# Two transformer blocks on one core: convolution steps of the vector engine issued in front of vector instructions that the kernel's own clock sees waiting

## The chip, the cores and the metric

The kernel runs on one core of one Trainium2 chip. The metric is the device time of one execution in microseconds (us); the median over several runs counts. Engines are named as the profile names them: PE (the matrix engine; PEld is its weight load), DVE (the vector engine), ACT (the scalar engine), POOL, SP (it issues most DMAs).

## The reference, cut to what matters

512 tokens of width 1024 go through two blocks. The first has a hybrid mixer (mLSTM and state space) and a convolutional feed-forward network; the change does not touch it. The second block begins with the stage that matters here:

```python
y = rmsnorm(h, norm_mix_g[l]) @ w_in[l]
q = partial_rotary(y[..., 0:D_ATT]...)          # 8 heads of 64
k = partial_rotary(y[..., D_ATT:2 * D_ATT]...)
v = y[..., 2 * D_ATT:3 * D_ATT]...
att = dilated_sliding_attention(q, k, v)
conv = conformer_conv(y[..., c0:c0 + D_CONV], y[..., c0 + D_CONV:c0 + 2 * D_CONV], ...)
h = h + jnp.concatenate([att, conv], axis=-1) @ w_out[l]
xk = (mn @ w_xk[l])...                           # keys and values of a memory of 256 tokens
xv = (mn @ w_xv[l])...
```

`conformer_conv` gates its input (a * sigmoid(g)), runs a depthwise convolution of 31 taps along the tokens, then a layer norm and a silu. Its result and that of the attention are the two halves of the input to `w_out`.

## The kernel before

The program is written out once, instruction by instruction, in Python; each engine then runs its instructions in the order in which they were written. Matrix products in fp32 quality are split: a weight block `raw` (128x1024) comes by DMA, ACT rounds it to `whi`, DVE writes the rest `wlo = raw - whi`, and activations are split the same way (`hh`/`hl`, `cath`/`catl`, `mnh`/`mnl`, `qkh`/`qkl`). Five weight blocks fit in the ring, so ACT makes a `whi` when PE has finished with the block five earlier.

What is written next is decided while the program is built. A class `Pace` keeps a modelled clock per engine: every call goes through `Engine.issue` (L342), which issues the instruction and then lets `Pace.note` (L297) advance the engine's clock to the time at which the operands are there, plus a cost. Foreground loops (`phaseB`, `phaseA`, `tokensA`) write matrix products. After every few of them `pump()` (L665) goes through a list of background generators and writes the next piece of each that is due: its operands are there by the model, and the modelled clock of its engines is at most a limit ahead of PE's. `fill()` and `flush()` write the weight splits.

The stage around the change stands from L2018 on. In the foreground: the convolution's input (`ag`), Q, K and V, the memory's keys and values (`w_xk_2`, `w_xv_2`), and `residual_rms("w_out_2", ...)` (L2072). In the background: `to_heads` (transposes and splits of Q and K), eight generators `dilated` (one head each; PE writes scores `p` into a bank of tag `at`, of which there are two, DVE adds `band` and takes the row maximum into `P`, ACT takes the exponent, PE transposes, and PE multiplies `PT` by `va`), `conv_array` (some even shifts of two of the four channel tiles, on PE, from `cuh`, `cul` and `dg`), and `conv31` (L1826):

```python
for n, d in enumerate(vec):
    w = col("conv_w", (15 + d) * 4 + ct)
    o, a = shifted(y, v, d)
    stt(o, a, w, o, op0=OP.mult, op1=OP.add)     # one convolution step
    ...
    if n % CONV_N == CONV_N - 1 or n == len(vec) - 1:
        yield
```

One step is one DVE instruction `cv<-a,cols,cv`; there are 106 of that form. After the last step comes the tail: PE transposes `cv` to tokens (`cva`), DVE takes mean and variance (`st`, `mv`), POOL the root (`rstd`), ACT normalizes `cva`, PE transposes back, ACT and DVE apply gain, tanh and gate, and split the result into `cath` and `catl`, the second half of `w_out`'s input. `conv31` is added with a limit of 2500 ns (`CONV_BACK`): `pump` writes no step while DVE's modelled clock is more than that ahead of PE's.

Of the kernel before, what the change touches and what calls it, by code (L numbers as in the profile page):

```python
# [68 lines left out]
CONV_AHEAD = 2  # L69
CONV_AT = 5  # L70
CONV_LATE = 2500.0
TOP = 0
RESTART = 0.0
ATT_AHEAD = 4

# [204 lines left out]
class Pace:  # L280
# [3 lines left out]
    def __init__(self):  # L284
        self.clock = {"PE": 0.0, "DVE": 0.0, "ACT": 0.0, "POOL": 0.0, "DMA": 0.0}
        self.wrote, self.read = {}, {}

    def when(self, a, eng="PE"):
        t, by = self.wrote.get(_name(a), (0.0, eng))
        if by == eng == "PE":  # L290
            return 0.0
        return t + LAG[by] + (100.0 if eng == "PE" else 0.0)
# [1 line left out]
    def ready(self, aps):  # L294
        return max([self.when(a) for a in aps] or [0.0])

    def note(self, eng, cost, outs, ins):  # L297
        t = max([self.clock[eng]] + [self.when(a, eng) for a in ins])
        for a in outs:
            for e in (() if eng == "PE" else (self.wrote.get(_name(a)),)) + (self.read.get(_name(a)),):  # L300
                if e and e[1] != eng:
                    t = max(t, e[0] + WAR * LAG[e[1]])
        if BANKED:
            for a in ins:
                e = self.read.get(_name(a))
                if e and e[1] != eng and _name(a).startswith("p_"):
                    t = max(t, e[0] + LAG[e[1]])
        t += cost
        self.clock[eng] = t
        for a in ins:  # L310
            self.read[_name(a)] = max(self.read.get(_name(a), (0.0, eng)), (t, eng))
        for a in outs:
            self.wrote[_name(a)] = (t, eng)


def _name(a):
    t = getattr(a, "tensor", None)
    return getattr(t if t is not None else a, "name", None)


def _is_ap(a):
    return hasattr(a, "shape") and _name(a) is not None


def _free(a):
    n = 1
    for k in tuple(a.shape)[1:]:
        n *= int(k)
    return n


class Engine:
# [5 lines left out]
    def __getattr__(self, name):  # L338
        call = getattr(self._eng, name)
        kind, pace = self._kind, self._pace  # L340

        def issue(*args, **kw):  # L342
            r = call(*args, **kw)  # L343
            aps = [a for a in args if _is_ap(a)] + [v for k, v in kw.items() if k != "accum_out" and _is_ap(v)]
            outs, ins = aps[:1], aps[1:]
            if _is_ap(kw.get("accum_out", 0)):
                outs = outs + [kw["accum_out"]]
            if name == "dma_start":
                n = _free(aps[0]) * int(tuple(aps[0].shape)[0]) * 4
                pace.note("DMA", n / 330.0, outs, ins)  # L350
                return r
            n = max(_free(a) for a in aps[:2]) if name in ("bn_stats", "tensor_reduce") else _free(aps[0])
            scal = sum(1 for a in ins[1:] if _free(a) == 1)
            if kind == "PE":
                fp32 = ins[0].dtype == F32
                if name == "transpose":
                    cost = 109.0
                elif fp32:
                    cost = 4.0 * max(n / 2.4 + 2.5, 27.0) * (0.5 if _free(ins[0]) == 64 else 1.0)
                else:  # L360
                    cost = n / 2.4 + 2.5 if n >= 256 else 213.0
            elif kind == "DVE":
                fast = name in ("tensor_scalar", "tensor_copy") and all(not _name(a).startswith("p_") for a in aps)
                cost = 66.0 + 61.0 * scal + n / (1.92 if fast else 0.96)
            elif kind == "ACT":
                cost = 80.0 + 93.0 * scal + n * 0.833
            else:
                cost = 520.0 if name == "tensor_tensor" else 100.0 + n
            pace.note(kind, cost, outs, ins)
            return r  # L370

        return issue
# [12 lines left out]
def two_blocks_kernel(ctx: ExitStack, tc: tile.TileContext, x, mem, wg, cols_d, rows_d, b_ada, s5p, wqk, small_d,  # L385
                      dil_d, rope_d, out, dbg=None, stop=None):
    pace = Pace()
# [14 lines left out]
    def uid(n):  # L402
        serial[0] += 1
        return f"{n}_{serial[0]}"

    def slot(name, dt=F32, w=512):
        return slots.tile([128, 520], dt, name=uid(name), tag="s")[:, :w]
# [16 lines left out]
    def f(ap):  # L424
        return ap.bitcast(F32)
# [28 lines left out]
    class Stream:  # L454
# [26 lines left out]
        def step(self):  # L481
            self._dma()
            e = PLAN[self.prep]
            t = self.raw.pop(self.prep)
            self.prep += 1
            if e[0] == "R":
                self._ada(e[1], e[2], [t[:, 512 * c:512 * c + 512] for c in range(2)])
                self.raws -= 1
            elif e[0] == "C":
                self._columns(e[1], e[2], t)  # L490
            else:
                ring = self.rings < RING
                if ring:
                    hi = wpool.tile([128, 1024], F32R, name=uid("whi"), tag="whi")
                    lo = wpool.tile([128, 1024], F32R, name=uid("wlo"), tag="wlo")
                    if len(self.when) >= RING:
                        pace.read[_name(hi)] = pace.read[_name(lo)] = (self.when[-RING], "PE")
                    act(hi, t, AF.Copy)
                    self.late.append((lo, t, f(hi), True))
                    hi, lo = ([v[:, 512 * c:512 * c + 512] for c in range(2)] for v in (hi, lo))  # L500
                    self.when.append(0.0)
                    self.rings += 1
                else:
                    hi, lo = ([slot("whs", F32R) for _ in range(2)] for _ in range(2))
                    for c in range(2):
                        act(hi[c], t[:, 512 * c:512 * c + 512], AF.Copy)
                    for c in range(2):
                        self.late.append((lo[c], t[:, 512 * c:512 * c + 512], f(hi[c]), c == 1))
                    self.extras += 1
                self.ready.append((e, hi, lo))  # L510
                self.out.append(len(self.when) - 1 if ring else None)
                if self.eager or LATE > 1e8:
                    self.flush(-1)
            self._dma()
# [106 lines left out]
    background, waiting, limit, loads = [], {}, {}, {}  # L621

    def add(g, backlog=BACKLOG, engines=("DVE", "ACT")):
        background.append(g)
        waiting[g], limit[g], loads[g] = None, backlog, engines
        return g
# [3 lines left out]

    def step(g):
        waiting[g] = None
        try:
            waiting[g] = next(g)
        except StopIteration:
            background.remove(g)
            del waiting[g]

    def vacant(tag):

        if len(banks[tag]) < BANKS[tag]:
            return 0.0
        o = banks[tag][-BANKS[tag]]
        t, by = max(pace.read.get(o, (0.0, "PE")), pace.wrote.get(o, (0.0, "PE")))
        return t + LAG[by] + 100.0

    def due(g):

        need = waiting[g]
        if callable(need):  # L650
            return 0.0 if need() else None
        if not need:
            return 0.0
        t = pace.ready([a for a in need if not isinstance(a, str)])
        return max([t] + [vacant(a) for a in need if isinstance(a, str) and a in BANKS])

    filler = []

    def top():

        for g in filler:
            while g in background and due(g) == 0.0 and busy(g) <= pace.clock["PE"] + limit[g]:
                step(g)

    def pump():  # L665
        moved = True
        while moved:
            moved = len(ws.ready) < FIRST and ws.fill()
            for g in list(background):
                t, pe = due(g), pace.clock["PE"]  # L670
                now = pe + SLACK
                if isinstance(waiting[g], list) and waiting[g][-1] in ("DVE", "ACT"):
                    now = max(now, pace.clock[waiting[g][-1]] + LEAD)
                if t is None or t > now or busy(g) > pe + limit[g]:
                    continue
                step(g)
                moved = True
                top()
                if RESTART and pace.clock["PE"] > pe + RESTART:
                    break  # L680
            moved = ws.fill() or moved
# [878 lines left out]
    for e in MIXER:  # L1560
        kind, i = e[0], int(e[1])
# [456 lines left out]
    ws.eager = "A" in EAGER  # L2018
    add(conv_array(), CONV_BACK)
    conv = add(conv31(), CONV_BACK, CONV_ON)  # L2020
    if TOP:
        filler.append(conv)
    for n, e in enumerate(ORDER2):
        if n == CONV_AT:
            limit[conv] = CONV_LATE
# [191 lines left out]
```

## Time and profile before

| | |
|---|---|
| time, median of 3 runs | 1681.92 us (1680.43 to 1681.93) |
| profiled execution, its own time | 1682.57 us |
| its span (first to last instruction) | 1680.8 us |
| PE busy | 1604.9 us, 95% |
| PE weight load busy | 1295.3 us, 77% |
| DVE busy | 988.2 us, 59% |
| ACT busy | 698.8 us, 42% |
| share of PE in the chain that ended last | 82% |

The span is 1.8 us shorter than the profiled execution's time; what lies around it is not in the trace. "Busy" counts an engine as busy while at least one of its instructions runs. In the page's strip of 40 slices one slice is 42 us.

### The profile page before, as it was taken

The page shows a single profiled execution, that of the slowest core. Times are in us where ns is not written, and L with a number is a line of the kernel's source. Part 1 is how long each engine was busy: PE and PEld are TensorE (multiplying, and loading weights), DVE is VectorE, ACT ScalarE, POOL GpSimd, SP SyncE. Part 2 cuts the span into 40 slices and gives each one's busy share as a digit, 9 for nine tenths or more (in the row PEclk, how much of TensorE's full clock was granted, in tenths as well). Part 3 has the DMA queues.
Part 4 walks back from the last instruction along what each step waited for, and adds up shares of the span by engine and source line. Part 5 has one row for each costly group of instructions (what it writes and reads, how often), then busy time and mean ns, then how long its engine had stood idle before and what let it go on. Part 6 is the DMA issues. An engine that isn't in the chain of part 4 may idle for free.

```text
span 1680.8 us, 20291 instructions
## 1 busy us (share of the span) xinstructions
PE 1604.9 (95%) x7788; PEld 1295.3 (77%) x7788; DVE 988.2 (59%) x1940; ACT 698.8 (42%) x1151; POOL 35.4 (2%) x59
## 2 busy tenths in 40 slices
PE   5999999999979999999989999976999999999998
PEld 3778777878868888888868877745888888888886
DVE  6687768687675365554585685475554543334343
ACT  4455644533253254223344446534644532323231
POOL 1000000000010000000010000000000000000000
PEclk9999999999989999999989999996999999999999
DMA  9322322474502343333422122320311323232321
GB/s 359 127 82 63 120 78 87 163 233 155 200 26 88 126 164 112 114 102 97 138 64 76 63 64 89 113 88 26 110 57 60 113 88 100 88 101 88 100 75 51
DMA packets 60953, 178.47 MB, mean 106 GB/s; under 512 B 6964, under 2 KB 12340, under 8 KB 60856
## 3 DMA queue, kind: packets, MB, share of 16 engines
q1 hardware_dynamic: 54288, 166.15, 30.4%
q10 hardware_dynamic: 6568, 11.02, 1.9%
q8 instruction: 61, 1.00, 0.3%
q14 instruction: 36, 0.29, 0.1%
HBM read 171.90 MB, written 5.24 MB: 105 GB/s over the span
## 4 chain that ended last, share of the span: by engine, by line
PE 82%; DVE 7%; ACT 3%; issue 2%; DMA 2%; ACTq 0%; POOL 0%; SPq 0%; DVEq 0%; POOLq 0%
PE p L343 82%; DVE cv L343 1%; DMA raw<-in_wg_dram 1%; DVE mx L343 1%; DVE wlo L343 1%; ACT whi L343 1%; DVE hl L343 0%; DMA xres<-in_x_dram 0%; DVE xcv L343 0%; DVE st L343 0%; DVE m L343 0%; ACT xn L343 0%; ACT hh L343 0%; DVE s5t L343 0%; DVE acc L343 0%
## 5 line engine op out<-in xcount | busy, mean ns | idle before, releaser
L343 DVE TENSOR_TENSOR wlo<-raw,whi 128x1024 fp32r<-128x1024 f32 x244 | 297.4, 1223 | 346.1 <-ACT whi L343 345.8
L343 PE MATMUL p<-hh,whi 128*128 128x512 f32 (+1 forms) x1112 | 427.8, 385 | 0.0
L343 PE MATMUL p<-hh,wlo 128*128 128x512 f32 (+1 forms) x1112 | 418.2, 376 | 0.0
L343 PE MATMUL p<-hl,whi 128*128 128x512 f32 (+1 forms) x1112 | 416.9, 375 | 0.6 <-DVE hl L343 0.6
L343 ACT ACTIVATE whi<-raw 128x1024 fp32r<-128x1024 f32 x244 | 256.2, 1055 | 329.9 <-PE p L343 279.9
L343 PEld LDWEIGHTS p<-hl,whi 128*128 128x128 f32 x1112 | 210.7, 190 | 41.2 <-issue 1.7
L343 PEld LDWEIGHTS p<-hh,wlo 128*128 128x128 f32 x1112 | 210.2, 189 | 41.5
L343 PEld LDWEIGHTS p<-hh,whi 128*128 128x128 f32 x1112 | 210.5, 189 | 40.4 <-issue 2.7
L343 PE MATMUL p<-whi,fh 128*128 128x512 f32 x408 | 161.0, 395 | 0.0
L343 PE MATMUL p<-whi,fl 128*128 128x512 f32 x408 | 160.9, 394 | 0.0
L343 PE MATMUL p<-wlo,fh 128*128 128x512 f32 x408 | 160.6, 394 | 0.0
L343 PEld LDWEIGHTS p<-wlo,fh 128*128 128x128 f32 x408 | 76.7, 188 | 18.2
L343 PEld LDWEIGHTS p<-whi,fl 128*128 128x128 f32 x408 | 76.6, 188 | 18.2
L343 PEld LDWEIGHTS p<-whi,fh 128*128 128x128 f32 x408 | 76.6, 188 | 18.0 <-DVE facc L343 0.2
L343 DVE SCALAR_TENSOR_TENSOR cv<-a,cols,cv 128x511 f32<-128x511 f32 (+14 forms) x106 | 78.3, 740 | 2.4
L343 DVE SCALAR_TENSOR_TENSOR fg<-p,cols,fg 128x511 f32<-128x511 f32 (+1 forms) x44 | 32.9, 749 | 49.4 <-ACT fg L343 48.6
L343 DVE TENSOR_TENSOR mf<-p,mf 128x512 f32<-128x512 f32 x48 | 32.1, 685 | 29.0 <-PE p L343 29.0
L343 ACT ACTIVATE junk<-mf 128x512 f32<-128x512 f32 x32 | 20.2, 630 | 65.9 <-DVE mf L343 65.9
L343 ACT ACTIVATE fg<-p,cols 128x512 f32<-128x512 f32 x22 | 17.1, 778 | 60.5 <-PE p L343 60.5
L343 PE MATMUL p<-small,xn 128*128 128x128 f32 x128 | 20.0, 295 | 22.2 <-DVE hl L343 8.7
L343 PE MATMUL p<-whi,hh 128*128 128x512 f32 x96 | 39.3, 409 | 0.0
L343 DVE SCALAR_TENSOR_TENSOR acc<-raw,silu_c,acc 128x512 f32<-128x512 f32 x56 | 38.6, 744 | 0.9 <-DMA raw<-in_wg_dram 0.9
(408 smaller groups left out, 2458.8 us busy)
## 6 DMA issues: line engine op xcount, KB each, us to landing
raw<-in_wg_dram SPq DMA_DIRECT2D x283, 512.0 KB, 3.6
rw<-in_wg_dram SPq DMA_DIRECT2D x32, 256.0 KB, 5.9
x<-in_x_dram SPq DMA_DIRECT2D x8, 256.0 KB, 5.3
xres<-in_x_dram ACTq DMA_DIRECT2D x8, 256.0 KB, 5.0
out_dram<-mf SPq DMA_DIRECT2D x8, 256.0 KB, 2.1
u_dram<-us ACTq DMA_DIRECT2D x4, 256.0 KB, 3.6
U<-u_dram SPq DMA_DIRECT2D x16, 64.0 KB, 4.0
wqk<-in_wqk_dram ACTq DMA_DIRECT2D x4, 256.0 KB, 2.9
```

Of the source, the lines that this page charges most:

```text
L343: r = call(*args, **kw)
```

## The change

`Engine.issue` now asks, before it issues a DVE instruction, how long DVE's modelled clock would stand still until that instruction's operands are there (`Pace.start`, split off from `note`). While that is over 600 ns (`GAP`), and the convolution's next step has its operands, the step is written first. The limit against PE's clock does not apply there. A generator that is itself being run is left alone. The switch `TOP`, which was off, is removed.

```diff
-TOP = 0
+GAP = 600.0
...
+    def start(self, eng, outs, ins):
...
+    def note(self, eng, cost, outs, ins):
+        t = self.start(eng, outs, ins) + cost
...
         def issue(*args, **kw):
-            r = call(*args, **kw)
             aps = [a for a in args if _is_ap(a)] + [v for k, v in kw.items() if k != "accum_out" and _is_ap(v)]
             outs, ins = aps[:1], aps[1:]
...
+            if kind == "DVE" and pace.idle:
+                pace.idle(lambda: pace.start(kind, outs, ins) - pace.clock[kind])
+            r = call(*args, **kw)
...
+    filler, gaps = [], []
+    within = []
+
+    def idle(wait):
+
+        if within:
+            return
+        within.append(1)
+        for g in gaps:
+            while g in background and due(g) == 0.0 and wait() > GAP and g not in running:
+                step(g)
+        within.clear()
...
     conv = add(conv31(), CONV_BACK, CONV_ON)
-    if TOP:
-        filler.append(conv)
+    gaps.append(conv)
```

All instructions of the program are the same ones, in the same number and sizes, on every engine. What differs is their order, from the last part of the convolution's input stage to the first half of `w_out`. The three places that follow are named by the tiles: `cv` is a channel tile of the convolution, `P` one tile of scores of a head, `wlo` a weight block, `ao` an attention output. (L343 became L353.)

On DVE before, the end of the convolution stands behind the last attention output; these are consecutive rows, from the last `ao` on, and 19 more steps follow them without a break:

```order
L343 TENSOR_TENSOR ao_9370<-p_9361,rs_9357 128x512
L343 TENSOR_TENSOR catl_9373<-ao_9370,cath_9372 128x512
L343 SCALAR_TENSOR_TENSOR cv_7700<-a_1382_7530,cols,cv_7700 128x500
L343 SCALAR_TENSOR_TENSOR cv_7700<-a_1382_7530,cols,cv_7700 128x499 x2
L343 TENSOR_TENSOR wlo_9387<-raw_9206,whi_9386 128x1024
L343 SCALAR_TENSOR_TENSOR cv_7700<-a_1382_7530,cols,cv_7700 128x498 x2
L343 SCALAR_TENSOR_TENSOR cv_7700<-a_1382_7530,cols,cv_7700 128x497 x2
L343 SCALAR_TENSOR_TENSOR cv_7985<-a_1396_7618,cols,cv_7985 128x511
L343 TENSOR_TENSOR wlo_9422<-raw_9235,whi_9421 128x1024
L343 SCALAR_TENSOR_TENSOR cv_7985<-a_1396_7618,cols,cv_7985 128x511
L343 SCALAR_TENSOR_TENSOR cv_7985<-a_1396_7618,cols,cv_7985 128x509 x2
```

On DVE in the changed kernel the last step (shape 128x497) stands between two score tiles of the seventh head, with a step in front of almost every score tile:

```order
L353 TENSOR_TENSOR wlo_8864<-raw_8506,whi_8863 128x1024
L353 ISA P_8880,sm_8838<-p_8876,band_7221 128x512
L353 ISA sm_8838 128x1
L353 TENSOR_SCALAR sm_8838<-sm_8838 128x1
L353 SCALAR_TENSOR_TENSOR cv_7854<-a_1396_7620,cols,cv_7854 128x498
L353 ISA P_8916,sm_8838<-p_8912,band_7222 128x512
L353 ISA sm_8838 128x1
L353 TENSOR_SCALAR sm_8838<-sm_8838 128x1
L353 SCALAR_TENSOR_TENSOR cv_7854<-a_1396_7620,cols,cv_7854 128x497 x2
L353 TENSOR_TENSOR wlo_8931<-raw_8657,whi_8930 128x1024
L353 ISA P_8962,sm_8838<-p_8958,band_7223 128x512
```

Counted over the whole program: before, 55 steps stand ahead of the first score tile on DVE, 11 between the first and the last of the 32, and 40 behind the last; in the changed kernel 69, 37 and none. Between the first step and that last step stand 20 `wlo` instructions; the next is the 21st.

On PE before, the transposes of `cv` stand behind the last product of `w_out` that needs only the attention (`cath_9372` is the last attention output), all 16 in one piece:

```order
L343 MATMUL p_9377<-whi_9202,cath_9372 128x512
L343 MATMUL p_9377<-wlo_9203,cath_9372 128x512
L343 MATMUL p_9377<-whi_9202,catl_9373 128x512
L343 MATMUL p_9452<-small,cv_7516 128x128
L343 MATMUL p_9452<-small,cv_7519 128x128
L343 MATMUL p_9452<-small,cv_7700 128x128
L343 MATMUL p_9452<-small,cv_7985 128x128
```

On PE in the changed kernel they stand in groups of four between products of the memory's values (`mnh`, `mnl`) and transposes of the last head's `P`:

```order
L353 MATMUL p_9297<-small,cv_7516 128x128
L353 MATMUL p_9297<-small,cv_7519 128x128
L353 MATMUL p_9297<-small,cv_7703 128x128
L353 MATMUL p_9297<-small,cv_7854 128x128
L353 MATMUL p_9194<-whi_9180,mnh_5386 128x512
L353 MATMUL p_9194<-wlo_9181,mnh_5386 128x512
L353 MATMUL p_9194<-whi_9180,mnl_5390 128x512
```

Behind the fourth such group come, before the first transpose of `cva`: 24 products of 128x512, four transposes of `P`, four small products of `rs`, and the eight products `PT` by `va` of the last pair of heads. From there to the first product with the convolution's `cath`: the 16 transposes of `cva` and 30 products of 128x512.

## Rows read from the trace of the kernel before

**Rows 1.** The page: busy time of each engine, and PE's granted clock in 40 slices.
```profile
PE 1604.9 (95%) x7788; PEld 1295.3 (77%) x7788; DVE 988.2 (59%) x1940; ACT 698.8 (42%) x1151; POOL 35.4 (2%) x59
PEclk9999999999989999999989999996999999999999
```
**Rows 2.** Stretches: length, busy us (instructions) of PE, PEld, DVE, ACT, POOL, clock, DMA.
```profile
880.00:1121.40 241.40, 241.40 (x1288) 188.83 (x1288) 150.45 (x298) 120.14 (x229) 0.00 (x0) 1.00 0.25 82
1121.40:1160.40 39.00, 12.64 (x43) 8.72 (x42) 27.24 (x43) 14.89 (x22) 1.01 (x1) 0.56 0.07 25
1160.40:1201.80 41.40, 41.40 (x224) 35.40 (x223) 17.77 (x32) 20.67 (x39) 3.12 (x4) 1.00 0.27 87
```
**Rows 3.** Timeline of PE: start, length, instruction, count [idle before, until what].
```profile
1121.36 0.38 PE L343 MATMUL p<-small,cv 128*128 128x128 f32 x2
1123.68 0.33 PE L343 MATMUL p<-small,cv 128*128 128x128 f32 x1 [1.94 <-ACT cv L343]
1142.46 3.13 PE L343 MATMUL p<-small,cv 128*128 128x128 f32 x13 [18.45 <-ACT cv L343]
1149.71 0.48 PE L343 MATMUL p<-small,cva 128*128 128x128 f32 x1 [4.12 <-ACT cva L343]
...
1155.67 0.79 PE L343 MATMUL p<-whi,cath 128*128 128x512 f32 x1 [0.81 <-ACT cath L343]
```
**Rows 4.** Timeline of DVE: the 21st `wlo`, and the last convolution steps.
```profile
1060.95 1.22 DVE L343 TENSOR_TENSOR wlo<-raw,whi 128x1024 fp32r<-128x1024 f32 x1 [2.10 <-ACT whi L343]
...
1124.59 17.06 DVE L343 SCALAR_TENSOR_TENSOR cv<-a,cols,cv 128x511 f32<-128x511 f32 x22
...
1161.62 0.69 DVE L343 TENSOR_TENSOR catl<-cv,cath 128x512 fp32r<-128x512 f32 x1 [0.70 <-ACT cath L343]
```
**Rows 5.** Timeline of PE at full clock: eight transposes, their successor; products after the hole.
```profile
1080.37 1.04 PE L343 MATMUL p<-small,P 128*128 128x128 f32 x8
1081.33 0.49 PE L343 MATMUL p<-qkh,qkh 64*128 64x512 f32 x1
...
1160.35 0.39 PE L343 MATMUL p<-whi,cath 128*128 128x512 f32 x1
...
1161.05 0.39 PE L343 MATMUL p<-whi,cath 128*128 128x512 f32 x1
```
**Rows 6.** Stretches, for instructions on `cv` alone: PE, PEld, DVE, ACT, clock, DMA.
```profile
895.00:988.00 93.00, 0.00 (x0) 0.00 (x0) 40.72 (x55) 3.23 (x5) 1.00 0.27 85
988.00:1060.00 72.00, 0.00 (x0) 0.00 (x0) 7.34 (x10) 0.71 (x1) 1.00 0.23 74
1060.00:1121.40 61.40, 0.04 (x1) 0.18 (x2) 11.85 (x17) 0.00 (x0) 1.00 0.32 104
1121.40:1142.00 20.60, 0.67 (x3) 0.23 (x2) 18.42 (x25) 1.04 (x2) 0.62 0.14 47
```
**Rows 7.** Stretches ahead of the hole, all instructions, columns as in Rows 2.
```profile
895.00:940.00 45.00, 45.00 (x215) 37.44 (x214) 30.84 (x39) 19.89 (x36) 0.00 (x0) 1.00 0.30 93
940.00:988.00 48.00, 48.00 (x226) 38.92 (x224) 40.48 (x93) 20.05 (x40) 0.00 (x0) 1.00 0.24 78
988.00:1060.00 72.00, 72.00 (x423) 54.42 (x422) 40.92 (x104) 46.20 (x96) 0.00 (x0) 1.00 0.23 74
```
**Rows 8.** Waits, 895 to 1121.4: who waited for what, us in total, times, longest.
```profile
DVE wlo L343 <- ACT whi L343: 40.7, 24, 5.8
ACT P L343 <- DVE sm L343: 27.1, 22, 2.2
...
DVE P L343 <- PE p L343: 7.9, 10, 1.9
```

More of the change, by code (lines that the diff above doesn't have):

```diff
@@ L286, in __init__ @@
         self.wrote, self.read = {}, {}
+        self.idle = None
     def when(self, a, eng="PE"):
@@ L295, in ready @@
         return max([self.when(a) for a in aps] or [0.0])
-    def note(self, eng, cost, outs, ins):
+    def start(self, eng, outs, ins):
         t = max([self.clock[eng]] + [self.when(a, eng) for a in ins])
@@ L307, in note @@
                     t = max(t, e[0] + LAG[e[1]])
-        t += cost
+        return t
+    def note(self, eng, cost, outs, ins):
+        t = self.start(eng, outs, ins) + cost
         self.clock[eng] = t
@@ L632, in step @@
         waiting[g] = None
+        running.append(g)
         try:
@@ L637, in step @@
             del waiting[g]
+        finally:
+            running.remove(g)
     def vacant(tag):
@@ L655, in due @@
         return max([t] + [vacant(a) for a in need if isinstance(a, str) and a in BANKS])
-    filler = []
+    filler, gaps = [], []
[8 more added lines that the diff above has]
+        within.clear()
+    running = []
+    pace.idle = idle
     def top():
```

## The prediction

> **What bounds the kernel now.** I read the page first: PE is busy for 1604.9 of 1680.8 us, and the granted clock falls below full speed in only a few of the 40 slices, the deepest in the slice from 1134 to 1177 us [rows 1]. So PE sets the time nearly everywhere, and what an off-path change on DVE can give is PE's idle time. The second view is the split into stretches. From 880 to 1121.4 us PE is busy in all of 241.4 us at clock 1.00 while DVE works 150.45 us; from 1160.4 on it is busy all the time again. Between them lie 39 us in which PE does 12.64 us of work at a mean clock of 0.56 [rows 2]. That hole is the object of the forecast.
>
> The third view is PE's timeline through the hole. At 1121.36 PE has nothing left but transposes of `cv`; the fourth channel tile is not there. It waits 18.45 us until 1142.46 for ACT's last pass over `cv`, then 4.12 us for `cva`, and 0.81 us for `cath`, with which the products of `w_out` go on at 1155.67 [rows 3]. The wait named after ACT is DVE's: 22 convolution steps run in one piece from 1124.59, 17.06 us long, or 0.775 us a step [rows 4]. Of the 106 steps 25 lie inside the hole and only 27 between 988 and 1121.4 [rows 6], though DVE stood idle in 24 places ahead of a `wlo`, 40.7 us in all, between 895 and 1121.4 [rows 8]. The work that fills the hole existed earlier, and so did the room.
>
> **The change, part by part.** No instruction is added or removed, so only places count. By the order of instructions, 40 steps leave the end: 14 now stand ahead of the first score tile, 26 among the score tiles. The last step stands just ahead of the 21st `wlo`, whose twin ran at 1060.95 us before [rows 4], 60 us ahead of the hole. PE's transposes of `cv` stand among the products of the memory's values. Three terms follow.
>
> First, what the hole gives back. It runs from 1121.36 to 1160.35, where products reach their full pace, 38.99 us. What PE must still do of it: 32 transposes of `cv` and `cva`, and the first nine products of `w_out` with `cath`. At full clock eight transposes took 0.96 us, from 1080.37 to the next start at 1081.33, so 0.12 each and 3.84 for all; three products took 0.70 us from 1160.35 to 1161.05, so 0.233 each and 2.10 for nine [rows 5]. The gain is 38.99 - 3.84 - 2.10 = 33.05 us. Of it 2.6 us are the nine products alone, which ran at half rate behind the hole (1155.67 to 1160.35 is 4.68 us).
>
> Second, the tail behind the last step (statistics, root, normalization, gate, split). Its cover is the work that PE now has beside it. Before, PE's own part took 7.25 us from the first transposes of `cv` to the first of `cva` (1142.46 to 1149.71), 5.96 us on to the first product, and 12.6 us from 1149.71 to the end of the last `catl` at 1162.31 [rows 3, 4]. In the changed order there stand between the last transposes of `cv` and the first of `cva` 24 products (5.6 us), four transposes (0.5), four `rs` products and eight of `PT` by `va`; taking these twelve at no more than an ordinary product (2.8), that is 8.9 us, against the 7.25 that were needed. To the first product with the convolution's `cath` follow 16 transposes and 30 products (1.9 + 7.0 = 8.9 us, against 5.96), and to the last two `cath` 24 products more (14.5 us, against 12.6). So I cost the tail at nothing. If that cover were gone, the stretch from 1142.46 to 1160.35 would stay (a rival below).
>
> Third, what the moved steps push back. All 40 take 40 x 0.775 = 31.0 us of DVE's time. Idle there is 14.16, 7.52 and 31.08 us in the three stretches from 895 to 1060, 52.8 in all [rows 7], so the room is there, but not to spare before 988: 14 steps, 10.9 us, go into 21.7. PE sees a late DVE in two ways. A `wlo` is made as soon as a ring place comes free, while blocks made earlier still wait for PE; one block serves 24 products of 0.233 us in most of these stages, 5.6 us, so a delay of a step or two is covered there. A score tile has less: its bank and the exponent hang on it; ACT waited for DVE's maximum in 22 of 32 tiles, and DVE for PE in only 10 [rows 8]. A step goes in only where the modelled wait is over 0.6 us and takes 0.775, so if the model's clock is right the instruction behind it comes at most 0.175 us later, 7.0 us for all 40 if every one reached PE; if the model is wrong everywhere, 31.0; if covered, 0. PE did not stand still in that stretch before, while DVE waited 24 times for a `whi` and ACT 22 times for a maximum, so the order has slack for both, and I take a value nearer the low end, 2.5 us.
>
> The profiled execution took 1682.57 us, 0.65 over the median of 1681.92. 1682.57 - 33.05 + 2.5 = 1652.0, against the median 1651.4 us. With the term between 0 and 7.0 the likeliest case covers 1648.9 to 1655.9.
>
> **The rivals.** *The tail stays open* (chance 0.10): the steps come early, but PE finishes attention before the tail's nine hand-overs between PE, ACT, DVE and POOL are done. Then only the part from 1121.36 to 1142.46 closes, 21.1 us less three transposes: 1682.57 - 20.7 - 0.65 = 1661.2. For it speaks the thin margin of 14.5 against 12.6 us; against it, that 12.6 was measured with PE at half clock.
>
> *DVE becomes the bound in the attention* (0.12): if the 26 steps fall between 988 and 1060 it goes from 40.92 to about 61 of 72 us [rows 7], and steps stand in front of nearly every score tile. If a third of the 40 reach PE in full, that costs 10.3 us instead of 2.5: 1659.2; up to two thirds, 1669.6. It would show as idle time of PE in front of products of `qkh` or transposes of `P`, released by DVE or ACT.
>
> *No change* (0.03): every moved step reaches PE in full. [...] Then 31.0 of the 33.05 us are lost: 1682.57 - 33.05 + 31.0 - 0.65 = 1679.9. Against it: the steps have a modelled wait behind them each, and the `wlo` have the blocks made earlier as a cover. [...]
>
> *Slower* (0.03): the same, and PE's waits come in pieces long enough to lower its clock, as the hole did; twice more, at the 2.6 us that nine products lost behind the hole, gives 1679.9 + 5.2 = 1685.1. It decides from 33.05 us of new loss on, 43 steps' worth.
>
> That the change doesn't do what it says is excluded by the order of instructions.
>
> **Chances and range.** The likeliest case has 0.72. From 1647, a little under the sum with no new wait, to 1662, which takes in the open tail and the milder half of the DVE case, lie some 0.87; what is left out is above it. 0.2% of the time, about what a measurement here can tell from no change, is 3.4 us: faster 0.94, within 0.03, slower 0.03.
>
> **What would show it.** Right: PE's idle 18.45 us in front of `cv` is gone; the clock stays at 1.00 from 880 to 1200; the last step runs near 1060 to 1070 us; the stretch from 880 to the end of the first half of `w_out` is 33 us shorter, less what PE waits in it. The step on the tail is wrong if PE waits in front of `cva` or `cath`; the one on the moved steps if PE has idle time between 895 and 1121 released by `P`, `sm`, `qkl` or `wlo`. The forecast as a whole fails if such waits add up to over 10 us, or if the stages behind `w_out` now wait for `raw`: before, the stream of weights had the hole to get ahead in, though it moved only 25 GB/s there against 82 ahead of it [rows 2], which is why I give this no term.

## The result, and the profile after

The changed kernel takes 1644.45 us (median of four runs, 1642.62 to 1646.0) against 1681.93 us before; the ratio is 0.9778, 95% interval 0.9761 to 0.9795. That is 37.5 us, 7.0 more than the 30.5 forecast, and below the low end of the range, 1647. The profiled execution took 1643.37 us with a span of 1641.5.

The page first: PE's busy time, and its granted clock in 40 slices, to be read against [rows 1].

```profile
PE 1591.2 (97%) x7788; PEld 1287.6 (78%) x7788; DVE 986.6 (60%) x1940; ACT 698.0 (43%) x1151; POOL 35.4 (2%) x59
PEclk8999999999989999999998999999999999999999
```

The slice with clock 6 is gone. PE was busy 13.7 us less with the same 7788 products, and the span is 39.3 shorter, so 25.6 us of idle time went as well. The chain that ended last has this piece now, in order of time (start, us, what):

```profile
877.81 284.27 PE p L353 x1552
...
1162.11 0.85 ACT hh L353 x2
```

From the first product of the second block to the end of `w_out` the chain does not leave PE. The same work took from 879.46 to 1201.80 us before. It is 38.0 us shorter; the rest of the 39.3 is 1.65 us ahead of it, where the two programs are the same, and -0.4 behind it. The stretches of the changed kernel, with the columns of [rows 2], answer to [rows 7]:

```profile
895.00:940.00 45.00, 45.00 (x208) 37.11 (x207) 38.04 (x49) 25.08 (x53) 0.00 (x0) 1.00 0.29 94
940.00:988.00 48.00, 48.00 (x227) 39.03 (x226) 44.90 (x100) 17.10 (x25) 0.00 (x0) 1.00 0.24 77
988.00:1060.00 72.00, 72.00 (x441) 55.42 (x441) 60.36 (x135) 48.00 (x101) 0.00 (x0) 1.00 0.24 81
...
877.80:1162.10 284.30, 284.29 (x1554) 227.46 (x1555) 194.93 (x372) 154.60 (x290) 4.14 (x5) 1.00 0.27 85
```

From 988 to 1060 DVE works 60.36 of 72 us instead of 40.92, and PE still does not wait; its clock is 1.00 throughout. For the instructions on `cv` alone, with the columns of [rows 6]: 69 steps run ahead of 988 us and the other 37 by 1060, and PE's 16 transposes take 2.40 us at full clock:

```profile
895.00:988.00 93.00, 0.00 (x0) 0.00 (x0) 51.16 (x69) 3.95 (x6) 1.00 0.26 85
988.00:1060.00 72.00, 0.00 (x0) 0.00 (x0) 27.12 (x37) 1.41 (x2) 1.00 0.24 81
1060.00:1121.40 61.40, 2.40 (x16) 1.96 (x16) 4.66 (x7) 7.65 (x12) 1.00 0.33 103
```

DVE's timeline at its last step (two instructions, the row answers to [rows 4]), and PE's timeline from the last transposes of `cv` to those of `cva`, which answers to [rows 3]:

```profile
1050.43 1.50 DVE L353 SCALAR_TENSOR_TENSOR cv<-a,cols,cv 128x497 f32<-128x497 f32 x2
1053.88 1.23 DVE L353 TENSOR_TENSOR wlo<-raw,whi 128x1024 fp32r<-128x1024 f32 x1 [1.95 <-ACT whi L353]
```

```profile
1098.73 0.60 PE L353 MATMUL p<-small,cv 128*128 128x128 f32 x4
1099.16 0.60 PE L353 MATMUL p<-small,P 128*128 128x128 f32 x4
...
1109.85 1.03 PE L353 MATMUL p<-small,cva 128*128 128x128 f32 x8
1110.64 0.47 PE L353 MATMUL p<-whi,cath 128*128 128x512 f32 x1
...
1116.72 0.60 PE L353 MATMUL p<-small,cva 128*128 128x128 f32 x4
1117.08 0.48 PE L353 MATMUL p<-whi,cath 128*128 128x512 f32 x1
```

No row carries a wait. Eight transposes take 0.79 us to the next start, 0.10 each. The waits between 895 and 1121.4, against [rows 8], show what the steps used up:

```profile
ACT P L353 <- DVE sm L353: 26.0, 17, 2.2
DVE wlo L353 <- ACT whi L353: 24.0, 22, 4.5
...
DVE P L353 <- PE p L353: 1.8, 2, 1.2
```

To see where the 38.0 us came from I added up, for each kind of product, the time from its start to the next start on PE, from the first product with `dg` to the last of `w_out`:

| us | before | after |
|---|---|---|
| transposes of `cv`, with the waits ahead of what follows | 28.35 | 1.66 |
| transposes of `cva` | 5.97 | 1.50 |
| products with `cath`, `catl` | 47.32 | 44.96 |
| 96 score products (`qkh`, `qkl`) | 25.21 | 21.31 |
| all | 270.19 | 232.10 |

The first three give 33.52 us: the hole, forecast at 33.05. The fourth gives 3.90, and no step of the prediction has it. All other kinds together give the remaining 0.67. PE's timeline in the changed kernel shows what it is. A score tile is three products; a head has 64 rows, and the two heads of a pair lie in the two halves of the 128 rows of one tile ("64*128"). There are three forms:

```profile
989.79 0.51 PE L353 MATMUL p<-qkh,qkh 64*128 64x512 f32 x2
990.13 0.40 PE L353 MATMUL p<-qkl,qkh 64*128 64x512 f32 x2
990.37 0.40 PE L353 MATMUL p<-qkh,qkl 64*128 64x512 f32 x2
990.70 0.50 PE L353 MATMUL p<-whi,hh 128*128 128x512 f32 x1
...
1066.03 0.50 PE L353 MATMUL p<-qkh,qkh 64*128 64x512 f32 x1
...
1066.83 0.39 PE L353 MATMUL p<-qkh,qkh 64*128 64x512 f32 x1
...
1067.63 0.50 PE L353 MATMUL p<-whi,mnh 128*128 128x512 f32 x1
...
1071.48 0.50 PE L353 MATMUL p<-qkh,qkh 64*128 64x512 f32 x1
...
1072.38 0.50 PE L353 MATMUL p<-whi,mnh 128*128 128x512 f32 x1
```

One tile alone takes 0.90 us to the next start (1071.48 to 1072.38), two of the same head, one behind the other, 1.60 (1066.03 to 1067.63). Two of the two heads of a pair take 0.91 for all six products (989.79 to 990.70), and the rows count each kind twice at one time: by the trace the two of a kind start 0.01 us apart. Such a pair is worth 1.80 - 0.91 = 0.89 us, two tiles of one head 0.2. In the order of instructions there are 3 pairs of 16 possible before and 8 in the changed kernel, and 3 and 1 neighbours of one head: 5 x 0.89 - 2 x 0.2 = 4.05, against the 3.90 added up.

### The profile page after: what moved, and what is told of

Read it like the earlier page. It is cut to its first block, busy times and chain, and to the rows that moved or that the text cites. A ratio compares the mean times of both kernels' runs of the same rounds, so it can differ in the third digit from the quotient of the medians.

```text
span 1641.5 us, 20288 instructions
## 1 busy us (share of the span) xinstructions
PE 1591.2 (97%) x7788; PEld 1287.6 (78%) x7788; DVE 986.6 (60%) x1940; ACT 698.0 (43%) x1151; POOL 35.4 (2%) x59
## 4 chain that ended last, share of the span: by engine, by line
PE 89%; DVE 4%; ACT 2%; issue 1%; DMA 1%; SPq 0%; POOL 0%; ACTq 0%; DVEq 0%; POOLq 0%
PE p L353 89%; DVE mx L353 1%; DMA raw<-in_wg_dram 1%; DVE wlo L353 0%; ACT whi L353 0%; DVE hl L353 0%; ACT xn L353 0%; ACT hh L353 0%; DVE acc L353 0%; DVE mf L353 0%; DVE st L353 0%; DVE gab L353 0%; ACT junk L353 0%; ACT us L353 0%; SPq L353 0%
## 5 line engine op out<-in xcount | busy, mean ns | idle before, releaser
L353 DVE TENSOR_TENSOR wlo<-raw,whi 128x1024 fp32r<-128x1024 f32 x244 | 297.7, 1224 | 331.4 <-ACT whi L353 330.9
L353 PE MATMUL p<-hh,whi 128*128 128x512 f32 (+1 forms) x1112 | 427.0, 384 | 0.0
L353 PE MATMUL p<-hl,whi 128*128 128x512 f32 (+1 forms) x1112 | 417.0, 375 | 0.7 <-DVE hl L353 0.7
L353 PE MATMUL p<-hh,wlo 128*128 128x512 f32 (+1 forms) x1112 | 417.3, 375 | 0.0
L353 ACT ACTIVATE whi<-raw 128x1024 fp32r<-128x1024 f32 x244 | 256.4, 1055 | 321.8 <-PE p L353 261.9
L353 PEld LDWEIGHTS p<-hh,wlo 128*128 128x128 f32 x1112 | 209.8, 189 | 41.3
L353 PEld LDWEIGHTS p<-hl,whi 128*128 128x128 f32 x1112 | 210.2, 189 | 40.9 <-issue 1.7
L353 PEld LDWEIGHTS p<-hh,whi 128*128 128x128 f32 x1112 | 210.0, 189 | 41.1 <-issue 2.7
L353 PE MATMUL p<-whi,fh 128*128 128x512 f32 x408 | 161.0, 395 | 0.0
L353 PE MATMUL p<-whi,fl 128*128 128x512 f32 x408 | 160.7, 394 | 0.0
L353 PE MATMUL p<-wlo,fh 128*128 128x512 f32 x408 | 160.5, 393 | 0.0
L353 PEld LDWEIGHTS p<-whi,fl 128*128 128x128 f32 x408 | 76.6, 188 | 18.3
L353 PEld LDWEIGHTS p<-whi,fh 128*128 128x128 f32 x408 | 76.6, 188 | 18.1 <-DVE facc L353 0.2
L353 PEld LDWEIGHTS p<-wlo,fh 128*128 128x128 f32 x408 | 76.6, 188 | 18.0
L353 DVE SCALAR_TENSOR_TENSOR cv<-a,cols,cv 128x511 f32<-128x511 f32 (+14 forms) x106 | 78.3, 739 | 2.2
L353 DVE SCALAR_TENSOR_TENSOR fg<-p,cols,fg 128x511 f32<-128x511 f32 (+1 forms) x44 | 33.0, 749 | 49.4 <-ACT fg L353 48.6
L353 DVE TENSOR_TENSOR mf<-p,mf 128x512 f32<-128x512 f32 x48 | 32.2, 686 | 28.9 <-PE p L353 28.9
L353 ACT ACTIVATE junk<-mf 128x512 f32<-128x512 f32 x32 | 20.2, 631 | 65.8 <-DVE mf L353 65.8
L353 ACT ACTIVATE fg<-p,cols 128x512 f32<-128x512 f32 x22 | 17.1, 778 | 60.5 <-PE p L353 60.5
L353 PE MATMUL p<-small,xn 128*128 128x128 f32 x128 | 20.2, 297 | 22.2 <-DVE hl L353 8.7
L353 ACT ACTIVATE fh<-sq 128x512 fp32r<-128x512 f32 x32 | 20.2, 632 | 45.0 <-DVE sq L353 45.0
L353 DVE SCALAR_TENSOR_TENSOR acc<-raw,silu_c,acc 128x512 f32<-128x512 f32 x56 | 38.7, 746 | 0.3 <-DMA raw<-in_wg_dram 0.3
```

## The experiments

Two theories stood at the start. **Order:** the surplus is the pairs, and the hole is worth what was forecast. **Hole:** the surplus comes from the hole, its clock of 0.56 [rows 2] above all, and the neighbourhood of score products does nothing. The first four kernels have either no pair or all 16, each with and without the change.

**No pairs, with the change.** A score tile is not written directly behind another.

```diff
+            while True:
                 yield [qh, ql, kh, kl, "at"]
+                if pace.pe != mark[0]:
+                    break
+                yield lambda: pace.pe != mark[0]
...
             PE.matmul(p, q2, kh, start=False, stop=True)
+            mark[0] = pace.pe
```

> The changed kernel, in which a head's score tile is not written directly behind a score tile of another head: some other PE instruction must stand between them. Nothing is left out. Of the 8 places where six score products of the two heads of a pair stand in one piece, none is left; the 106 convolution steps stand as in the changed kernel (69, 37, 0). Theory (the gain that the prediction missed comes from such places, where the six products took 0.90 us instead of twice 0.89): 8 x 0.88 = 7.0 us slower than the changed kernel, 1651.5, with no hole. Rival (the missed gain comes from waits of PE that the order before had hidden in its busy time, and pairs have no part in it): no change, 1644.5.

Measured: 1656.41 us (1655.78 to 1657.38), ratio to before 0.9853, 0.984 to 0.9866. The score products' busy time (columns: length, PE busy, clock, DMA) and PE's waits from 878 to 1170:

```profile
895.00:1121.40 226.40, 30.73 (x96) 1.00 0.26 89
```

```profile
PE p L354 <- ACT cva L354: 1.2, 3, 0.8
PE p L354 <- ACT rs L354: 1.2, 1, 1.2
PE p L354 <- ACT cath L354: 0.6, 1, 0.6
```

The changed kernel has 22.91 us in the place of 30.73. Here new waits do appear, 3.06 us in all, in the tail and at the last heads. The run is 12.0 us slower than the changed kernel, where the theory had 7.0: from start to start the score products take 7.2 us more (28.50 against 21.31), the waits are 3.1, and 1.7 stay open.

**All 16 pairs, with the change.** The even head's generator writes the score tiles of both heads; both banks must be free.

```diff
+                yield [qh, ql, kh, kl, "at2"]
+                for i in range(2):
                     p = bank("at")
+                    r_ = slice(64 * i, 64 * i + 64)
...
+                    PE.matmul(p, q1, kh[r_], start=True, stop=False)
+                    PE.matmul(p, q1, kl[r_], start=False, stop=False)
+                    PE.matmul(p, q2, kh[r_], start=False, stop=True)
```

> The changed kernel, in which one generator writes the score tiles of both heads of a pair, so all 16 places hold six products in one piece. Nothing is left out; convolution steps 69, 37, 0. Theory of the pairs: 8 more places at 0.88 us, 7.0 us faster than the changed kernel, 1637.4. Rival: no change, 1644.5, or slower, since both banks of the scores must be free at once: 16 waits of PE at the length of one score evacuation, 0.69 us, would be 11 us slower, 1655.

Measured: 1640.06 us (1639.21 to 1641.51), ratio 0.9756, 0.9743 to 0.9769. Its score products:

```profile
895.00:1121.40 226.40, 15.53 (x96) 1.00 0.27 89
```

The score products take half of what they take without pairs; what PE gains there it partly gives back in waits, 3.22 us from 895 to 1121.4, so the run stays 2.7 us above the theory's 1637.4.

**The same two edits without the change.**

> The kernel before, with no steps in front of waiting instructions, but with all 16 pairs in one piece (3 before). Nothing is left out. By the order 20 convolution steps stand behind the last score tile instead of 40, so part of the hole closes as well. Theory: 13 pairs at 0.88 us give 11.4 us, 1670.5; with the hole shorter by up to 20 x 0.775 = 15.5 us, down to 1655. The score products alone should take 16 x 0.90 = 14.4 us instead of 25.2. Rival (no effect of pairs): 1681.9, or 1666 by the hole alone, with the score products still at 25 us.

> The kernel before, with no pair left (3 before) and the convolution steps as they were (55, 10, 41). Nothing is left out. Theory: 3 x 0.88 = 2.6 us slower than before, 1684.6, and against the first run of this set, which has no pair either, 33 to 34 us slower: the hole alone, 33.05 by the prediction's first term. Rival (the hole alone is worth the whole 37.5 us): 1682 here and 37.5 us between the two.

Measured with 16 pairs: 1657.51 us (1655.97 to 1660.24), ratio 0.9861, 0.9847 to 0.9874. Measured with none: 1687.83 (1684.87 to 1688.91), ratio 1.0038, 1.0025 to 1.005. Between no pairs and all, the score products' time from start to start goes from 28.50 to 14.59 us with the change: 13.91 / 16 = 0.87 a pair. With 0.2 for each neighbour of one head, 28.50 - 0.87 x 3 - 0.6 = 25.3 for the kernel before and 28.50 - 0.87 x 8 - 0.2 = 21.3 for the changed one, against 25.21 and 21.31. The 0.87 comes from neither of these two kernels, and for the kernel before the 0.2 doesn't either, so the theory of the order stands.

It also gives the price of the change by itself. With no pair on either side it is 1687.83 - 1656.41 = 31.4 us, less than the 33 to 34 that I had expected and far from the rival's 37.5. The prediction's sum was 33.05 - 2.5 = 30.55, but that the two lie so close is in part luck: the changed kernel without pairs has 3.06 us of waits in its time, and the changed kernel itself has none. One limit of these four: the whole order is planned anew, and without the change the pairs move convolution steps as well (31 instead of 11 among the score tiles in the kernel with 16 pairs). So its hole is smaller, and the change is worth only 17.5 us there.

**Half of the change at a time.** Steps go into gaps only behind the first score tile, or, with `within or begun` in the second kernel, only ahead of it.

```diff
-        if within:
+        if within or not begun:
...
             p = bank("at")
+            begun.append(1)
```

> The changed kernel, in which steps go in front of waiting vector instructions only from the first score tile on: one part of the change alone. Nothing is left out. Convolution steps 55, 51, 0 (ahead of, among and behind the score tiles; the changed kernel has 69, 37, 0), 5 pairs in one piece instead of 8. Theory (the hole closes as soon as no step stands behind the attention; pairs are worth 0.88 us each): hole closed, 1644.5 + 3 x 0.88 = 1647.1. Rival (the 14 early steps are needed, DVE has no room for 51 steps among the tiles): 14 x 0.775 = 10.9 us of new waits of PE, 1658.

> The changed kernel, in which steps go in front of waiting vector instructions only up to the first score tile: the other part alone. Nothing is left out. Convolution steps 69, 16, 21; 9 pairs. Theory: the hole stays for the steps behind the tiles and for the tail, as in the run of the kernel before with all pairs, which had 20 steps left and 14.7 us of waits of PE; so about 20 us slower than the changed kernel, 1665. Rival (moving any 14 steps is enough, since 15 steps found room behind the last tile before): hole closed, 1644.

Measured: 1649.53 us (1648.63 to 1652.19), ratio 0.9813, 0.9796 to 0.9829, for the first; 1658.88 (1656.3 to 1661.52), ratio 0.9865, 0.985 to 0.9879, for the second. The gaps among the score tiles take all 51 steps that were left and give 32.5 us, of which two more pairs are 1.7; PE waits 1.4 us for `cath`, and the run is 2.4 us above the theory. The gaps ahead of the tiles, taken alone, leave 21 steps behind the last score tile, and PE waits at the old place (timeline of PE in the second kernel):

```profile
1117.45 0.77 PE L353 MATMUL p<-small,cv 128*128 128x128 f32 x5 [1.00 <-ACT cv L353]
1118.88 1.39 PE L353 MATMUL p<-small,cv 128*128 128x128 f32 x8 [0.66 <-ACT cva L353]
1125.36 0.47 PE L353 MATMUL p<-small,cva 128*128 128x128 f32 x1 [5.08 <-ACT cva L353]
```

The tail then stands open, as in the first rival. That costs 14.4 us against the changed kernel, less than the 20 expected. Of its 23.1 us some 5 are pairs, 9 against 3. The halves do not add up (32.5 + 23.1 against 37.5), since either closes part of the same hole.

**The threshold at 0 and at 200 ns.** `GAP` is 0.0 or 200.0 instead of 600.0.

> The changed kernel with 0 in place of 600 ns: a step goes in front of every vector instruction that has any modelled wait. Nothing is left out. Steps 73, 33, 0; 4 pairs. Theory (pairs, and DVE's lateness is covered): 1644.5 + 4 x 0.88 = 1648.0, with no wait of PE. Rival (a step in front of a short wait holds up what stands behind it by nearly its whole length): each of some 40 steps up to 0.775 us, 1655 to 1675, with waits of PE released by DVE.

> The threshold is 200 ns instead of 600 (0 in the run that lost 19 us). By the order of instructions no step stands between reading a row maximum and the instruction that scales it, where 11 stood at 0 ns; 7 pairs of score products stand side by side, against 8 in the changed kernel and 4 at 0 ns. If the 11 steps inside that hand-over made the loss at 0 ns: the changed kernel's 1644.4 plus 0.9 for one pair, 1645, between 1643 and 1649, with no waits of PE for PT. Rival, a step in front of any short wait delays the attention, wherever it stands: 1650 to 1661, with PE waiting for PT, rs or cva.

Measured at 0: 1663.16 us (1662.32 to 1666.75), ratio 0.9894, 0.9879 to 0.9909. The time is the rival's, though ACT and not DVE released PE's waits. At 200: 1646.95 (1646.01 to 1647.23), ratio 0.9793, 0.978 to 0.9806. At 0 DVE's timeline has steps inside the hand-over from a row maximum to ACT:

```profile
1004.06 0.69 DVE L353 CUSTOM_DVE_ANT_0 P<-p,band 128x512 f32<-128x512 f32 x1 [0.23 <-PE p L353]
1004.68 0.08 DVE L353 DVE_READ_ACCUMULATOR2_ANT sm<- 128x1 f32 x1
1004.68 0.74 DVE L353 SCALAR_TENSOR_TENSOR cv<-a,cols,cv 128x507 f32<-128x507 f32 x1
1005.34 0.15 DVE L353 TENSOR_SCALAR sm<-sm 128x1 f32<-128x1 f32 x1
```

The scaled maximum comes 1.28 us behind the start of the maximum instead of 0.73; this happens in 11 of 32 tiles. The attention falls behind, the memory's products stand in PE's order in its place, and for the last heads nothing is left to put beside them (PE's timeline):

```profile
1078.73 0.40 PE L353 MATMUL p<-whi,mnl 128*128 128x512 f32 x1
...
1084.69 1.11 PE L353 MATMUL p<-small,P 128*128 128x128 f32 x4 [2.05 <-ACT PT L353]
...
1115.85 1.14 PE L353 MATMUL p<-small,P 128*128 128x128 f32 x8 [0.99 <-ACT PT L353]
1119.66 1.97 PE L353 MATMUL p<-small,cva 128*128 128x128 f32 x8 [2.67 <-ACT PT L353]
...
1132.98 0.50 PE L353 MATMUL p<-whi,cath 128*128 128x512 f32 x1 [2.18 <-ACT cath L353]
```

The first row is the last product of the memory's values; in the changed kernel such products run until 1100.77, beyond the last transposes of `P` at 1099.16. PE is idle for 10.0 us from 878 to 1160, the four pairs fewer cost some 3, and the granted clock falls as well, where the changed kernel has 1.00 (all PE work; length, busy, clock, DMA):

```profile
1060.00:1100.00 40.00, 37.95 (x167) 0.91 0.27 84
```

From 1060 to 1121 it is 0.92. By that clock some 5 us are lost (0.08 x 61.0, an estimate that counts idle time too).

At 200 ns no step stands in that hand-over, PE has no wait for `PT`, and 16 us come back. It still waits 1.5 us for `cath` and 1.2 for `rs`, which with one pair fewer is more than the 2.5 us that still lack against the changed kernel. That the eleven places made the loss is thereby made likely but not isolated, for the order differs elsewhere too.

**No limit at all, without the change.** Both limits of the convolution against PE's clock are removed in the kernel before.

```diff
-CONV_BACK = 2500.0
+CONV_BACK = 1e9
...
-CONV_LATE = 2500.0
+CONV_LATE = 1e9
```

> The kernel before, in which only the limit on the convolution is lifted (2500 ns to no limit); no step is put in front of a waiting instruction. Nothing is left out. All 106 steps then stand ahead of the first score tile; 8 pairs. 51 steps more ahead of the tiles are 39.5 us of DVE's time against 21.7 us of its idle time from 895 to 988. Theory (first in, first out: what stands behind the steps is late): hole closed, but DVE 18 us late at the start of the attention; PE waits for it up to that, 1645 to 1662, with the waits released by DVE near 940 to 1000. Rival (only the place behind the attention matters, any earlier place does): 1644.5.

Measured: 1701.05 us (1700.72 to 1702.82), ratio 1.0117, 1.0102 to 1.0132, slower than before, and I had expected it faster. DVE's timeline has 60 steps in one piece, and PE's timeline what waited behind them:

```profile
902.32 46.60 DVE L343 SCALAR_TENSOR_TENSOR cv<-a,cols,cv 128x511 f32<-128x511 f32 x60
948.84 0.68 DVE L343 SCALAR_TENSOR_TENSOR a<-th,a 128x512 f32<-128x512 f32 x1
```

```profile
927.02 0.79 PE L343 MATMUL p<-whi,hh 128*128 128x512 f32 x1 [7.52 <-ACT a L343]
...
955.38 0.79 PE L343 MATMUL p<-whi,hh 128*128 128x512 f32 x1 [22.87 <-ACT a L343]
```

PE waits 30.4 us for the banks of the convolution's own input. ACT reads them out (`a`), but in its order of instructions they stand behind instructions that wait for DVE's steps: the last pass over `cv`, and `cuh`, which needs the `a` that DVE writes at 948.84. A later channel tile does the same to `qka`, for which PE waits 19.0 us more (timelines of ACT and PE):

```profile
925.77 0.72 ACT L343 ACTIVATE cv<-cv,cols 128x512 f32<-128x512 f32 x1 [23.77 <-DVE cv L343]
...
949.56 0.63 ACT L343 ACTIVATE cuh<-a 128x512 fp32r<-128x512 f32 x1 [22.10 <-DVE a L343]
...
1003.09 0.72 ACT L343 ACTIVATE cv<-cv,cols 128x512 f32<-128x512 f32 x1 [17.06 <-DVE cv L343]
```

```profile
1004.34 0.79 PE L343 MATMUL p<-whi,hh 128*128 128x512 f32 x1 [15.96 <-ACT qka L343]
```

Behind the first two waits PE's products start 0.43 us apart instead of 0.23; the granted clock is 0.58 on average from 920 to 958, where the kernel before has 1.00. The hole is closed and a larger one opened, from some 200 us earlier on. So the gain is not in writing the steps early as such, it is in writing them where DVE stood idle.

**All pairs, and steps only into long gaps.** The kernel with 16 pairs, `GAP` at 1500.0.

> All 16 pairs side by side, and the threshold 1500 ns instead of 600, so that a step goes in only where the modelled wait is about twice a step. Of the convolution steps 6 come behind the last score tile instead of none. If the 3.2 us in which PE waits in the run with all pairs are made by steps in front of score tiles: those waits go, 1637. Rival, they are made by the attention's last heads running without other work for PE, and the six late steps add to them: 1640 to 1646.

Measured: 1645.68 us (1643.76 to 1647.16), ratio 0.9788, 0.9774 to 0.9801. The rival had it: PE's idle time from 895 to 1121.4 goes up from 3.22 to 6.71 us, at `cath`, `cva` and `rs`. The kernel with all pairs at 600 ns stays the fastest of the study, at 1640.06 us. Its interval overlaps that of the changed kernel (0.9743 to 0.9769 against 0.9761 to 0.9795); its score products took 6.7 us less from start to start, and new waits gave 3.2 of them back.

## Why the prediction was wrong in size

**What bounds the kernel** was right: a hole of PE behind the attention, opened by the convolution's steps on DVE. The mechanism was right too.

**The hole** was forecast at 33.05 us and gave 33.52: transposes cost 0.10 us each, not 0.12, and the products with `cath` gave back 2.36 us instead of 2.58. **The tail at nothing** was right: between the last transposes of `cv` and the first of `cva` PE had 11.1 us of other work (1098.73 to 1109.85) where 7.25 were needed. **The last step** ran at 1050 us, not at 1060 to 1070. In part that is a miscount: the row at 1060.95 in [rows 4] is the 22nd `wlo` behind the first step, and the 21st ran earlier (DVE before):

```profile
1056.67 1.22 DVE L343 TENSOR_TENSOR wlo<-raw,whi 128x1024 fp32r<-128x1024 f32 x1 [2.62 <-ACT whi L343]
```

**The new waits** were taken at 2.5 us and came out at nothing. The premise of the rival was met, DVE at 60.36 of 72 us where I had written about 61, and steps stood in front of many score tiles (of the 31 behind the first, 18 have one between themselves and the tile ahead; that is many, but not almost every one). Two things speak for why it cost nothing, and no run separates them. The maxima were hardly late: added up from the timelines of the two kernels without pairs, a maximum starts 0.82 us behind the end of its products with the change and 0.67 without, 4.9 us over 32 tiles. (In the changed kernel it is 1.40 against 0.62 before, but that goes with the pairs: with all 16 it is 2.30 with the change and 2.34 without.) And PE had products of the memory's keys and values beside the scores; where those end before the last heads do, without pairs (3.06 us) and at 0 ns (10.0 us), PE waits. The low end of the term, 0, was in the likeliest case's own range.

**The step that failed** is the first sentence of the part on the change: no instruction is added or removed, so only places count. I then priced places only by who waits for whom, and took a product's cost as the same wherever it stands. The score products cost 3.9 us less, since the new order puts 8 of 16 pairs of heads side by side instead of 3. The difference of 7.0 us is 2.5 (waits), 3.9 (pairs) and 0.5 (the hole), with 0.1 left over. That it closes so well is in part luck: the terms come from one profiled execution of each kernel, and those two differ by 39.2 us, the medians by 37.5. With 3.9 us for the pairs the low end would have been near 1643, and the time inside the range. The count could have been had beforehand, from the order of instructions; the price could not be read from [rows 5], which show one score product beside transposes. But it stood in the trace of the kernel before, in each of its three pairs (PE's timeline; a tile alone took 0.88 us there, from 989.98 to 990.86):

```profile
987.10 0.51 PE L343 MATMUL p<-qkh,qkh 64*128 64x512 f32 x2
...
988.00 0.44 PE L343 MATMUL p<-small,qka 128*128 128x128 f32 x2
```

The *no change* and *slower* rivals were wrong for this change, yet what they suppose did occur in another kernel: where there was no wait to fill, the steps delayed what stood behind them. In the run without a limit the `a` behind 46.60 us of steps starts only at 948.84, PE waits 30.4 us for ACT's `a` and 19.0 for `qka`, and its clock is 0.58 from 920 to 958.

## What to carry to other kernels

When a change only reorders, price the neighbourhoods as well as the waits: count on the matrix engine which instructions became neighbours, and look in the trace for places where such neighbours start together. Work that fills an engine's idle time belongs where the engine would wait anyway; the same steps put early without regard to that made this kernel slower, 1701.05 us against 1681.99. How long the wait must be was not sharp here: a threshold of 0.2 us cost 2.5 us against 0.6, a threshold of 0 cost 18.7, likely because steps then stood between the links of a short hand-over to another engine. The tail behind the last step cost nothing here, where PE had 11.1 us of other work to take first and 7.25 were needed, so look at where that other work ends.

## What the runs showed of the hardware

Score products of the two heads of a pair, whose operands lie in the two halves of their tiles' 128 rows, written one group behind the other into different banks, start together by the trace: in the changed kernel each kind twice within 0.01 us, at 989.79, 990.13 and 990.37. These six products of 512 columns take 0.91 us to the next start, against 1.60 us for six of one head and 2 x 0.90 = 1.80 for two tiles that stand alone; 1.80 / 0.91 = 1.98. Three products of the first head stand ahead of the second head's first in the order of instructions, so by their starts PE did not take these six in the order in which they were written. With all 16 pairs instead of none, the score products took 13.9 us less of 28.5.

In the traces of the kernels before and after, the first score product behind a product over all 128 rows, and the first product of 512 columns over all 128 rows behind a score product, start 0.33 to 0.35 us ahead of the next instead of 0.23 (of two heads side by side, ahead of the next kind). No run shows what causes that.
